# Rows and bases of matmul operands moved to multiples of 256 bytes in a one-layer hybrid decoder step

## The chip, the core and the metric

The kernel runs on one core of a Trainium2 chip. The metric is the device time of one execution in microseconds (us), lower is better. Engines are named as the profile names them: PE is TensorE's matmul, PEld its weight load, DVE is VectorE, ACT is ScalarE, POOL is GpSimd, SP is the engine that issues most DMAs.

## What is computed

One inference step of one layer of a decoder whose heads fall into three groups, for 256 prompt tokens and 8 sample tokens that are handled together (T = 264 columns):

```python
D_MODEL = 4096                       # D_IN = 13324, D_MIX = 4096
P = rmsnorm(h) @ W_in                # one combined projection
A: sliding-window attention (12 heads, 4 kv heads, window 128, sinks, ALiBi), times silu(z_a)
B: mLSTM matrix memory (6 heads, chunks of 64), per-head RMS norm, output gate, times silu(z_m)
C: chunked spatial gating u * (tril(W_s) v + b), times silu(z_c)
h = h + concat(A, B, C) @ W_out
y = rmsnorm(h) ; states of A, B and C are outputs too
```

Almost all of the arithmetic is in the two projections. They are multiplied in float32 precision: each operand is split into a high and a low part of type fp32r, and three of the four products are summed.

## The kernel before

**Tiling.** The 4096 rows of the contraction are 32 tiles of 128 partitions (KT = 32). The tokens, transposed, are the moving operand: tile `xh` holds the high parts and `xl` the low parts, each `[128, 32, 264]`, so that row `k` of either is 264 consecutive fp32r values (1056 bytes) in every partition. The weights are the stationary operand. The output columns are worked on in 34 groups of 512 columns (26 of `W_in`, then 8 of `W_out`). In a group the contraction goes in 16 steps `c` of two rows (KK = 2): rows 2c and 2c+1. Each step has a weight tile of 128 x 1024 values, which `load_w` (L214) brings into a buffer `wf` by one DMA of 512 KB on SP's queue, four steps ahead. `split_w` (L223), two steps ahead, makes `wh` (ACT) and `wl = wf - wh` (DVE) of it. `wf`, `wh` and `wl` have three buffers each.

**The matmuls.** In the main loop (L989) each step runs 24 matmuls: for four column tiles `j`, for the two rows, three products into the accumulator `mp` of that column tile.

```python
for j in range(4):
    for kk in range(KK):
        k = KK * c + kk
        s = slice(P * j, P * j + P)
        PE.matmul(out, wh[:, kk, s], xh[:, k], ...)   # the first argument after out is stationary
        PE.matmul(out, wh[:, kk, s], xl[:, k], ...)
        PE.matmul(out, wl[:, kk, s], xh[:, k], ...)
```

Each matmul streams 264 columns past a stationary block of 128 x 128, and each has a weight load of its own. There are 34 x 16 x 24 = 13056 of them. The profile shows them as `mp<-xh,wh`, `mp<-xl,wh` and `mp<-xh,wl`: the moving operand stands first.

**Around them.** The work of the three head groups is written as generators that the main loop resumes between column tiles (`tick`); what they put on PE are some 700 small matmuls and transposes in plain fp32. The order on every engine is that of the program text; the scheduler's own reordering is off. At the end of each group the accumulators are read by ACT and DVE (`evac`). After the last group, a norm factor is formed and `finish` (L1067) scales the result on DVE and POOL and writes it out.

**Memory.** The pool `const` (L94) hands out addresses in the order of the calls: `xh`, `xl`, `yb` (the tokens in fp32, later the residual), `sms` (small constants, among them the identity for transposes), `ones`, `rstd`, `acc` and some narrow ones. The pool with `wf`, `wh` and `wl` lies behind it. In front of everything lie 16384 bytes of scratch for DMAs whose descriptors are made on the chip by software, and a few constants. Nearly all instructions stand under line 201 in the profile, which is a helper that records every operation; they are told apart by their tiles.

Where the operands of the 13056 matmuls begin, in bytes from the start of a partition, in the built program:

| operand | begins at | one row or block further | position within 256 bytes |
|---|---|---|---|
| `xh`, row k | 16512 | + 1056 per row | (128 + 32 k) mod 256 |
| `xl`, row k | 50304 | + 1056 per row | (128 + 32 k) mod 256 |
| `wh`, three buffers | 137248 | + 2048 per kk, + 512 per j | 32, always |
| `wl`, three buffers | 149536 | + 2048 per kk, + 512 per j | 32, always |

So the two rows of a step stand at 128 and 160 in steps 0, 4, 8 and 12 of a group, at 192 and 224 in steps 1, 5, 9 and 13, at 0 and 32 in steps 2, 6, 10 and 14, and at 64 and 96 in steps 3, 7, 11 and 15.

Of the kernel before, what the change touches and what calls it, by code (L numbers as in the profile page):

```python
# [10 lines left out]
F32 = mybir.dt.float32  # L11
F32R = mybir.dt.float32r
# [6 lines left out]
P = 128  # L19
D = 4096  # L20
KT = D // P
TP = 256
TS = 8
T = TP + TS
# [44 lines left out]
NWARM = 9  # L69
LAG = 6.0  # L70
NCH = KT // KK

SM = {}

# [14 lines left out]
def body(tc, xt, wi, wg, wo, sm, kc, vc, c0, wst, w00, bs, cgain, cbias,  # L89
         o_y, o_kv, o_cp, o_mp, o_cs, o_ms, o_cvp, o_cvs):  # L90
    nc = tc.nc
    from contextlib import ExitStack
    with ExitStack() as ctx:
        cp = ctx.enter_context(tc.tile_pool(name="const", bufs=1))  # L94
# [27 lines left out]
        ph.switch()  # L122
        keep = Phase("keep")

        xh = cp.tile([P, KT, T], F32R, name="xh")
        xl = cp.tile([P, KT, T], F32R, name="xl")
        yb = cp.tile([P, KT, T], F32, name="yb")
        sms = cp.tile([P, NSM], F32, name="sms")
        ones = cp.tile([P, P], F32, name="ones")
        epsc = cp.tile([P, 2], F32, name="epsc")  # L130
        epsc2 = cp.tile([P, 1], F32, name="epsc2")
        rstd = cp.tile([P, T], F32, name="rstd")
        acc = cp.tile([P, KK, T], F32, name="acc")

        def sc(name, i=0, n=None, rows=slice(None)):
# [74 lines left out]

        steps = [(g, c) for g in range(NG + NGO) for c in range(NCH)]
        wf_t, wh_t, wl_t = {}, {}, {}
# [23 lines left out]
        def load_x(s):  # L236
            if s < NCH:
                nc.sync.dma_start(yb[:, KK * s:KK * s + KK, :], xt[:, KK * s:KK * s + KK, :])

        def split_x(s):  # L240
            if s >= NCH:
                return
            for k in range(KK * s, KK * s + KK):
                if s == 0:
                    V.tensor_scalar(xh[:, k], yb[:, k], sc("ng", k), None, ALU.mult)
                else:
                    A.activation(xh[:, k], yb[:, k], AF.Copy, scale=sc("ng", k))
                V.scalar_tensor_tensor(xl[:, k], yb[:, k], sc("ng", k), xh[:, k].bitcast(F32),
                                       ALU.mult, ALU.subtract)

        SQ = [6, 7, 8, 9] + [s for s in range(NCH) if s not in (6, 7, 8, 9)]

        def square_x(n):

            if n >= NCH:
                return
# [732 lines left out]
        for n, (g, c) in enumerate(steps):  # L989
# [24 lines left out]
            for j in range(4):  # L1014
                tick()
                out = main_ps[j][:, :T]
                for kk in range(KK):
# [4 lines left out]
                    PE.matmul(out, wl[:, kk, s], xh[:, k], start=False, stop=(k == KT - 1))  # L1022
                if c == NCH - 1:
                    if g < NG:
# [151 lines left out]
```

## Time and profile before

| | |
|---|---|
| runs of the kernel | 1704.19 us median of three (1701.7 to 9350.31) |
| the profiled execution | 1703.58 us, its span 1701.9 us |
| mean granted TensorE clock | 0.994 |
| busy: PE, PEld | 1678.2 us, 1662.2 us |
| busy: DVE, ACT, POOL | 909.4 us, 739.2 us, 80.7 us |
| read from HBM, written | 314.20 MB, 12.60 MB: 192 GB/s over the span |

The span runs from the first to the last instruction that the profile records; the execution's own time is 1.7 us longer. A row of a group gives the instruction with its tiles and shapes, how many there are, their busy time and the mean of one, and the idle time ahead of them. The end of a matmul in the profile is modelled, and a row's duration (0.28 us) overlaps that of the next matmuls, so the pace is read from the starts. In the views in order of time the first column is the start in us from the start of the span, the second the duration.

### The profile page before, as it was taken

How to read it: one execution, taken by the hardware profiler on the slowest of the kernel's cores; microseconds unless marked ns; L12 is line 12 of the kernel's file. 1: busy time of each engine (PE TensorE's matmuls, PEld its weight loads, DVE VectorE, ACT ScalarE, POOL GpSimd, SP SyncE). 2: the span in 40 equal slices, each digit the busy share in tenths (PEclk: the TensorE clock that was granted, in tenths of full speed). 3: DMA queues.
4: the chain of work that ended last, by engine and by line, in shares of the span. 5: the costliest groups of instructions: out<-in, count | busy, mean ns of one | idle time of the engine just before them, and what ended most of it. 6: DMA issues, size and time to landing. Idle time of an engine off the chain costs nothing.

```text
span 1701.9 us, 32534 instructions
## 1 busy us (share of the span) xinstructions
PE 1678.2 (99%) x13754; PEld 1662.2 (98%) x13754; DVE 909.4 (53%) x1277; ACT 739.2 (43%) x971; POOL 80.7 (5%) x82
## 2 busy tenths in 40 slices
PE   9999999999999999999999999999999999999995
PEld 9999999999999999999999999999999999999995
DVE  6555644555544455555555665444666554444445
ACT  6554433444434343444344444334454444344442
POOL 0000000000000000001001100000100120000002
PEclk9999999999999999999999999999999999999998
DMA  8555558545455555667767666555656655555553
GB/s 297 169 177 175 185 185 276 157 157 162 149 173 176 183 177 183 203 202 234 228 212 240 214 223 216 180 180 180 206 176 221 206 185 188 186 177 183 177 182 145
DMA packets 102177, 328.91 MB, mean 193 GB/s; under 512 B 11090, under 2 KB 24328, under 8 KB 102032
## 3 DMA queue, kind: packets, MB, share of 16 engines
q1 hardware_dynamic: 101072, 326.04, 59.8%
q8 instruction: 107, 1.75, 0.4%
q10 hardware_dynamic: 960, 0.81, 0.1%
q14 instruction: 38, 0.31, 0.0%
HBM read 314.20 MB, written 12.60 MB: 192 GB/s over the span
## 4 chain that ended last, share of the span: by engine, by line
PE 97%; DVE 1%; DMA 1%; ACT 0%; issue 0%; SPq 0%; DVEq 0%; ACTq 0%
PE mp L201 93%; PE mx L201 3%; DVE yb L201 1%; DMA wf<-wo 1%; PE sn L201 0%; DVE wl L201 0%; DMA wf<-wi 0%; PE gps L201 0%; ACT wh L201 0%; DVE rstd L201 0%; DVE TM L201 0%; DVE mvs L201 0%; ACT L201 0%; DVE es L201 0%; SPq L973 0%
## 5 line engine op out<-in xcount | busy, mean ns | idle before, releaser
L201 PE MATMUL mp<-xh,wh 128*128 128x264 f32 x4352 | 1250.4, 287 | 1.7 <-ACT wh L201 1.1
L201 PE MATMUL mp<-xh,wl 128*128 128x264 f32 x4352 | 1238.8, 285 | 2.6 <-DVE wl L201 2.6
L201 PE MATMUL mp<-xl,wh 128*128 128x264 f32 x4352 | 1237.4, 284 | 0.0
L201 DVE TENSOR_TENSOR wl<-wf,wh 128x1024 fp32r<-128x1024 f32 (+1 forms) x545 | 686.4, 1263 | 756.8 <-ACT wh L201 750.4
L201 ACT ACTIVATE wh<-wf 128x1024 fp32r<-128x1024 f32 (+1 forms) x545 | 575.1, 1058 | 823.8 <-PE mp L201 737.5
L201 PEld LDWEIGHTS mp<-xh,wh 128*128 128x128 f32 x4352 | 819.7, 188 | 8.1 <-issue 5.5
L201 PEld LDWEIGHTS mp<-xh,wl 128*128 128x128 f32 x4352 | 819.9, 188 | 3.5 <-DVE wl L201 3.5
L201 PEld LDWEIGHTS mp<-xl,wh 128*128 128x128 f32 x4352 | 819.9, 188 | 0.4
L201 POOL TENSOR_TENSOR acc<-acc,es 128x264 f32<-128x264 f32 x29 | 21.9, 755 | 417.1 <-ACT es L201 415.1
L201 POOL TENSOR_SCALAR_AFFINE_SELECT tmp<-bc 128x128 f32<-128x128 f32 x12 | 5.5, 482 | 495.8 <-DMA bc<-gd 495.8
L201 ACT ACT_TABLE_LOAD x22 | 28.2, 1283 | 1.2 <-PEq L1156 0.8
L201 ACT ACTIVATE es<-yb 128x264 f32<-128x264 f32 x37 | 15.3, 412 | 17.7 <-DVE yb L201 17.7
L201 POOL TENSOR_TENSOR cb<-cb,bc 128x2056 f32<-128x2056 f32 x6 | 21.7, 3616 | 0.0
L201 ACT ACTIVATE bias<-bias,ar 128x128 f32<-128x128 f32 (+1 forms) x24 | 10.8, 448 | 24.9 <-DVE ar L201 24.8
L201 POOL MEMSET pad<- 128x1024 f32 x2 | 1.9, 950 | 413.7 <-PE mx L201 413.7
L201 DVE SCALAR_TENSOR_TENSOR cb<-vb,wsk,cb 128x257 f32<-128x257 f32 x48 | 20.1, 480 | 0.0
L201 ACT ACTIVATE es<-et 128x264 f32<-128x264 f32 x32 | 12.6, 419 | 17.1 <-DVE yb L201 13.9
L201 ACT ACTIVATE xh<-yb 128x264 fp32r<-128x264 f32 x32 | 12.1, 412 | 17.7 <-DVE yb L201 17.7
L201 DVE TENSOR_TENSOR et<-mp,rstd 128x264 f32<-128x264 f32 x52 | 18.8, 423 | 0.0
L201 ACT ACTIVATE yb<-yb,sms 128x264 f32<-128x264 f32 x32 | 16.5, 517 | 1.0
L201 DVE TENSOR_TENSOR yb<-yb,rstd 128x264 f32<-128x264 f32 x32 | 16.1, 558 | 0.0
L201 DVE SCALAR_TENSOR_TENSOR xl<-yb,sms,xh 128x264 fp32r<-128x264 f32 x32 | 14.4, 489 | 0.8 <-ACT xh L201 0.8
(177 smaller groups left out, 461.6 us busy)
## 6 DMA issues: line engine op xcount, KB each, us to landing
wf<-wi SPq DMA_DIRECT2D x415, 512.0 KB, 3.4
wf<-wo SPq DMA_DIRECT2D x128, 512.0 KB, 3.4
cb<-c SPq DMA_DIRECT2D x12, 514.0 KB
o_cs<-cb SPq DMA_DIRECT2D x12, 514.0 KB, 6.2
vb<-vsd SPq DMA_DIRECT2D x12, 512.0 KB, 4.8
yb<-xt SPq DMA_DIRECT2D x34, 132.0 KB, 3.5
yb<-xt SPq DMA_DIRECT2D x15, 264.0 KB, 7.1
o_y<-yb SPq DMA_DIRECT2D x7, 528.0 KB, 3.3
```

The source lines that it names most:

```text
L201: return fn(*a, **k)
```

## The change

Each row of `xh` and `xl` is given 320 values of room (1280 bytes, five times 256), of which the first 264 are used: the tile is `[128, 32, 320]` and the kernel keeps a view of 264 columns. Two small tiles that nothing reads or writes, of 128 and 96 bytes, are put in front of `xh` and in front of `acc`. The scratch for DMAs shrinks from 16384 to 1024 bytes, which makes room for the two larger tiles. `yb`, `mp` and all other tiles keep their shapes.

```diff
+ROW = 320
+PAD0, PAD1 = 32, 24
...
-        xh = cp.tile([P, KT, T], F32R, name="xh")
-        xl = cp.tile([P, KT, T], F32R, name="xl")
+        cp.tile([P, PAD0], F32, name="pad0")
+        xh = cp.tile([P, KT, ROW], F32R, name="xh")[:, :, :T]
+        xl = cp.tile([P, KT, ROW], F32R, name="xl")[:, :, :T]
         yb = cp.tile([P, KT, T], F32, name="yb")
...
         rstd = cp.tile([P, T], F32, name="rstd")
+        cp.tile([P, PAD1], F32, name="pad1")
         acc = cp.tile([P, KK, T], F32, name="acc")
...
-    nc = _bacc.Bacc("TRN2", target_bir_lowering=False, num_devices=1)
+    nc = _bacc.Bacc("TRN2", target_bir_lowering=False, num_devices=1, dynamic_dma_scratch_size=1024)
```

No instruction is added, removed or moved: every engine has the same operations in the same order and shapes. What changes are addresses. In the built program afterwards:

| operand | begins at | one row or block further | position within 256 bytes |
|---|---|---|---|
| `xh`, row k | 1280 | + 1280 per row | 0, always |
| `xl`, row k | 42240 | + 1280 per row | 0, always |
| `wf`, `wh`, `wl`, three buffers each | 124160, 136448, 148736 | + 2048 per kk, + 512 per j | 0, always |

`yb` moves from 84096 (128 within 256 bytes) to 83200 (0), `wf` from 32 to 0, `ones` from 0 to 128, the identity in `sms` from 232 to 104. The tiles of the head groups, behind these, all move down by 800 bytes and so stand 32 bytes lower within 256 than before (224 becomes 192, 96 becomes 64).

## The prediction

> **What bounds the kernel now.** I read the page's table of busy times first, then the groups of instructions, then the chain that ended last.
>
> ```profile
> span 1701.9 us, 32534 instructions
> PE 1678.2 (99%) x13754; PEld 1662.2 (98%) x13754; DVE 909.4 (53%) x1277; ACT 739.2 (43%) x971; POOL 80.7 (5%) x82
> ...
> PE 97%; DVE 1%; DMA 1%; ACT 0%; issue 0%; SPq 0%; DVEq 0%; ACTq 0%
> ...
> L201 PE MATMUL mp<-xh,wh 128*128 128x264 f32 x4352 | 1250.4, 287 | 1.7 <-ACT wh L201 1.1
> L201 PE MATMUL mp<-xh,wl 128*128 128x264 f32 x4352 | 1238.8, 285 | 2.6 <-DVE wl L201 2.6
> L201 PE MATMUL mp<-xl,wh 128*128 128x264 f32 x4352 | 1237.4, 284 | 0.0
> L201 DVE TENSOR_TENSOR wl<-wf,wh 128x1024 fp32r<-128x1024 f32 (+1 forms) x545 | 686.4, 1263 | 756.8 <-ACT wh L201 750.4
> L201 ACT ACTIVATE wh<-wf 128x1024 fp32r<-128x1024 f32 (+1 forms) x545 | 575.1, 1058 | 823.8 <-PE mp L201 737.5
> ```
>
> PE is busy nearly all the time, the chain lies on it for 97% of the span, and its three large groups wait for almost nothing (1.7, 2.6 and 0.0 us). The two engines that feed it are idle for long: ACT waits 737.5 us for PE to free a weight buffer. So the time is the number of matmuls, 3 x 4352 = 13056, times the pace at which PE starts them, and some 100 us of other work. The pace is not the mean of 284 to 287 ns, because successive matmuls overlap. It is read from a long undisturbed piece of the chain:
>
> ```profile
> 482.59 265.10 PE mp L201 x2172
> ```
>
> 265.10 us over 2172 matmuls are **122.0 ns** each, and 13056 x 0.1220 = 1593 us of the 1701.9. Nothing else in this kernel is worth a tenth of that, so the question is whether these 122.0 ns depend on addresses. For that I cut a quiet piece (in a group of the output projection, past its first steps) at the starts of four successive steps, which take their two rows of x from different places within 256 bytes: 128 and 160, then 192 and 224, then 0 and 32, then 64 and 96. The columns are the window, its length, PE's busy time and the matmuls that touch it (24 start in each), the clock and the share of DMA.
>
> ```profile
> 1548.04:1551.02 2.98, 2.98 (x26) 1.00 0.57 187
> 1551.02:1553.93 2.91, 2.91 (x26) 1.00 0.59 186
> 1553.93:1556.83 2.90, 2.90 (x26) 1.00 0.56 181
> 1556.83:1559.75 2.92, 2.92 (x26) 1.00 0.59 180
> ```
>
> The same 24 matmuls take 2.98, 2.91, 2.90 and 2.92 us: 124.2, 121.2, 120.8 and 121.7 ns each. The clock is full in all four and DMA alike, and the weights stand at 32 within 256 in all four. So the place of x costs up to 3 ns in 122, and at the worst place (128 and 160) the pace is the slowest. That much the trace shows. Within the third step the rows alternate in threes, and the first matmul of each three shows how long a row holds PE:
>
> ```profile
> 1553.93 0.28 PE L201 MATMUL mp<-xh,wh 128*128 128x264 f32 x1
> ...
> 1554.30 0.28 PE L201 MATMUL mp<-xh,wh 128*128 128x264 f32 x1
> ...
> 1554.66 0.28 PE L201 MATMUL mp<-xh,wh 128*128 128x264 f32 x1
> ...
> 1555.02 0.28 PE L201 MATMUL mp<-xh,wh 128*128 128x264 f32 x1
> ...
> 1555.38 0.29 PE L201 MATMUL mp<-xh,wh 128*128 128x264 f32 x1
> ...
> 1555.75 0.28 PE L201 MATMUL mp<-xh,wh 128*128 128x264 f32 x1
> 1555.88 0.28 PE L201 MATMUL mp<-xl,wh 128*128 128x264 f32 x1
> 1555.99 0.28 PE L201 MATMUL mp<-xh,wl 128*128 128x264 f32 x1
> 1556.12 0.28 PE L201 MATMUL mp<-xh,wh 128*128 128x264 f32 x1
> ...
> 1556.48 0.28 PE L201 MATMUL mp<-xh,wh 128*128 128x264 f32 x1
> ...
> 1556.84 0.29 PE L201 MATMUL mp<-xh,wh 128*128 128x264 f32 x1
> ```
>
> The row at 0 holds PE from 1553.93, 1554.66, 1555.38 and 1556.12 for 0.37, 0.36, 0.37 and 0.36 us, 121.7 ns per matmul. The row at 32 does so from 1554.30, 1555.02, 1555.75 and 1556.48 for 0.36, 0.36, 0.37 and 0.36 us, 120.8 ns, and three of the four give 120.0.
>
> **The change part by part.** *x at 0 instead of all eight places.* Two readings of these rows give two answers. If the place of x alone counts, all rows will run as the row at 0 does: 121.7 instead of 122.0 ns, a gain of 0.3 x 13056 = 4 us. If what counts is how x stands to the weight block that PE loads beside it, then the row at 32 is the one to look at: the weights are at 32 too, the difference is 0, and after the change it is 0 for every matmul (x at 0, weights at 0). I take the second, because the row with difference 0 is the quickest in its step and the step with the largest differences (96 and 128) the slowest. Between 120.0 and 120.8 I take 120.4: a gain of 1.6 x 13056 = **21 us**.
>
> *Weights at 0 instead of 32.* The trace of before has every main weight block at 32, so it shows nothing of this. By the nearest rows, those of x's places, a place is worth between 1.2 ns less (120.8) and 2.2 ns more (124.2) than the mean, so between -16 and +29 us. I take nothing for it, because with the difference held at 0 I have no row for either sign, and keep both ends for the range.
>
> *The small matmuls.* The remaining matmuls of PE, 13754 - 13056 = 698, have operands that move down by 32 within 256 bytes. At the largest spread seen, 3.4 ns, that is 2 us either way. I take 0.
>
> *DVE, ACT and DMA.* They read and write at other addresses: `wf` and `yb` now begin at 0. Whatever that does to `wl` (1263 ns) or `wh` (1058 ns) is hidden under a step of 2900 ns on PE: both have more idle time ahead of them than they are busy. DVE's 909.4 us are 1.7 us a step, so it would have to grow by over a microsecond a step before PE waited for it. In the first group the DMAs are near their limit:
>
> ```profile
> 20.00:40.00 20.00, 20.00 (x166) 20.00 (x166) 14.71 (x22) 14.03 (x24) 0.00 (x0) 1.00 0.94 321
> ```
>
> PE is busy in all 20 us there with DMA at a share of 0.94. A gain of 1.6 ns in 122 would ask for 1.3% more, which fits; a gain of 7 ns would not, and would be lost for the 16 steps of that group (16 x 24 x 7 ns = 2.7 us).
>
> *The smaller scratch.* The page lists DMA issues from SP and ACT alone, with the weights the largest group:
>
> ```profile
> q1 hardware_dynamic: 101072, 326.04, 59.8%
> ...
> wf<-wi SPq DMA_DIRECT2D x415, 512.0 KB, 3.4
> wf<-wo SPq DMA_DIRECT2D x128, 512.0 KB, 3.4
> ```
>
> None has descriptors that software makes, so nothing uses the scratch: 0, and no DMA that could run short of it.
>
> **Sum.** 1703.58 of the profiled execution - 21 = **1682 us**, 1.2% less. The profiled execution stands 0.6 us under the median of the runs, 1704.19, which is nothing beside the terms.
>
> **What a page says against it.** The Trainium skill, "SBUF — State Buffer", section "Who interferes with whom", gives PE two read ports of its own, one for the moving operand and one for weight loads, and says that PE never waits on anyone. By that no address matters and the time stays at 1704. The four windows above speak against it: with equal clock and DMA they differ by 0.08 us in 2.9 with the place of x alone.
>
> **The rivals.** *No change.* It would be so if the eight places of x are phases of one pattern whose mean of 122.0 ns is set by something else, such as the load of a weight block that each matmul needs. For it: no step comes out under 120.8 ns, and single gaps that are shorter are paid back by the next. At 121.7 to 122.0 ns the time is 1700 to 1704 us.
>
> *Faster by much.* The differences between places might be what is left of a stall that is present at all of them, and that only vanishes when x and weights both begin at 0. For it: in the row at 32 the gap from its second matmul to its third, 1555.88 to 1555.99, is 0.11 us; the second is the one of the three that has matmuls of its own row on both sides, and so the nearest thing to the stream after the change. Against it: the gaps beside it are 0.13, as if they paid for it. If 115 ns (between 0.11 and 0.12) became the pace, the gain is 7.0 x 13056 = 91 us, or 88 without the first group: 1615 us. It is faster by over 2% (34 us, 2.6 ns) from a pace of 119.4 ns down.
>
> The Trainium skill, "TensorE: Matmul & The Clock Gate", section "Back-to-back issue gap", gives N / 2.4 + 2.5 ns for isolated matmuls; at N = 264 that is 112.5, an estimate by which this rival would reach 1580 us. No stretch of this trace runs at that pace.
>
> *Slower.* With everything at 0, each matmul's read of x starts at the same place as the weight block that is read beside it, and if both are served by the same part of the memory, the collision comes in every matmul in the same way rather than in some. The rows at 128 and 160 show what a bad phase costs when it does not go away:
>
> ```profile
> 1549.53 0.29 PE L201 MATMUL mp<-xh,wh 128*128 128x264 f32 x1
> ...
> 1549.91 0.28 PE L201 MATMUL mp<-xh,wh 128*128 128x264 f32 x1
> ```
>
> 0.38 us for three, 126.7 ns: 4.7 x 13056 = 61 us more, 1765 us. At the pace of that whole step (124.2) it would be 29 us, 1732. Against it: the row at 32 has difference 0 already and is not slow. It decides from 124.6 ns on. About 2% is what a measurement of this kernel can tell from no change.
>
> **How the numbers follow.** Forecast (pace 119.4 to 121.6, 1670 to 1699 us): 0.44. No change (1699 to 1710): 0.11. Faster by much (under 1670): 0.33. Slower (over 1710): 0.12, of which a third stays within 2%. So faster by over 2% is 0.33 and 2 in 100 that the forecast is just too small, 0.35; slower by over 2% 0.08; within 2% the other 0.57. The predicted time is that of the forecast, 1682 us. The range has to take in most of the fast case and part of the slow one: from 1610, which is just under a pace of 115, to 1725, which covers a step's pace of 123.6. Outside I leave about 0.1 below and 0.08 above.
>
> **What would show it.** In the profile after, the steps of a quiet stretch would all be equally long, at 24 x 120.4 ns = 2.89 us, instead of 2.98, 2.91, 2.90 and 2.92 in turn. If they are equal at 2.92 or more, place counts but my choice of row was wrong. If they still alternate by fours, x's place was never the cause. Equal steps of 2.76 or less are the fast rival, 2.99 or more the slow one. DVE's and ACT's idle times should shrink by the gain and no DMA wait should appear on PE outside the first group. The prediction is wrong if the place of the weight block has an effect of its own, which no row of before can show, or if equal places make a stable pattern that the mixed sequence never reached.

## The result, and the profile after

The changed kernel takes **1690.01 us** in the median of four runs (1687.46 to 1692.27), against 1703.86 us for the kernel before in the same session: a ratio of **0.992**, 95% interval 0.990 to 0.994. That is 14 us or 0.8% less: within 2%, but clear of zero. The forecast was 1682. One of the four runs of the kernel before took 9350 us; it is left out of the ratio.

The page of the profile after (span, busy times, the large groups; the line numbers are four higher):

```profile
span 1687.7 us, 32534 instructions
PE 1663.3 (99%) x13754; PEld 1646.4 (98%) x13754; DVE 911.6 (54%) x1277; ACT 739.1 (44%) x971; POOL 80.9 (5%) x82
...
L205 PE MATMUL mp<-xh,wh 128*128 128x264 f32 x4352 | 1242.5, 286 | 2.5 <-ACT wh L205 1.9
L205 PE MATMUL mp<-xh,wl 128*128 128x264 f32 x4352 | 1231.3, 283 | 2.6 <-DVE wl L205 2.5
L205 PE MATMUL mp<-xl,wh 128*128 128x264 f32 x4352 | 1230.9, 283 | 0.0
L205 DVE TENSOR_TENSOR wl<-wf,wh 128x1024 fp32r<-128x1024 f32 (+1 forms) x545 | 685.3, 1261 | 741.1 <-ACT wh L205 734.5
L205 ACT ACTIVATE wh<-wf 128x1024 fp32r<-128x1024 f32 (+1 forms) x545 | 574.9, 1057 | 808.6 <-PE mp L205 712.1
```

The span is 14.2 us shorter, PE is busy 14.9 us less, and hardly anything else has moved: DVE's and ACT's busy times (within 2.2 us), their durations for `wl` and `wh`, and PE's waits are as before. The idle time ahead of `wl` and `wh` is shorter by 15.7 and 15.2 us. The same long undisturbed piece of the chain as before, 2172 matmuls, gives the pace:

```profile
478.24 262.90 PE mp L205 x2172
```

262.90 / 2172 = 121.0 ns instead of 122.0. How it comes about is seen in windows cut at the starts of successive steps, first in one group of the output projection, then in the next (24 matmuls start in each window):

```profile
1488.74:1491.62 2.88, 2.88 (x26) 1.00 0.70 218
1491.62:1494.50 2.88, 2.88 (x26) 1.00 0.62 188
1494.50:1497.38 2.88, 2.88 (x26) 1.00 0.58 182
...
1535.04:1537.95 2.91, 2.91 (x27) 1.00 0.61 200
1537.95:1540.86 2.91, 2.91 (x27) 1.00 0.60 186
1540.86:1543.77 2.91, 2.91 (x26) 1.00 0.57 180
```

The repeat after four steps is gone. But there are now two paces: 2.88 us a step (120.0 ns) in one group, 2.91 (121.3 ns) in the next, with the same instructions, addresses and clock. Over the whole trace, of the 469 steps that hold no small matmuls, some 200 take 2.88 us and some 220 take 2.91 or 2.92; the rest begin a group or wait. The order in time shows what the slower pace is:

```profile
1535.64 0.28 PE L205 MATMUL mp<-xh,wl 128*128 128x264 f32 x1
1535.77 0.28 PE L205 MATMUL mp<-xh,wh 128*128 128x264 f32 x1
1535.88 0.28 PE L205 MATMUL mp<-xl,wh 128*128 128x264 f32 x1
1536.01 0.28 PE L205 MATMUL mp<-xh,wl 128*128 128x264 f32 x1
1536.13 0.29 PE L205 MATMUL mp<-xh,wh 128*128 128x264 f32 x1
1536.25 0.28 PE L205 MATMUL mp<-xl,wh 128*128 128x264 f32 x1
1536.38 0.28 PE L205 MATMUL mp<-xh,wl 128*128 128x264 f32 x1
1536.49 0.28 PE L205 MATMUL mp<-xh,wh 128*128 128x264 f32 x1
```

The gaps, from starts rounded to 0.01 us, are 0.13, 0.11, 0.13, 0.12, 0.12, 0.13, 0.11: a pattern of five (126, 124, 116, 120 and 121 ns in turn, to within a nanosecond or so) that goes on until something interrupts PE. In the quicker groups the five are replaced by gaps of 120 ns, or by four of 123, 122, 120 and 115 ns, whose mean is 120.0 too. The trace changes from one pattern to the other only at the start of a group or at a step that waits or holds small matmuls. What decides which one comes next is not shown.

### The profile page after: what moved, and what is told of

It is laid out like the page before. It is cut to its first block, busy times and chain, and to the rows that moved or that the text cites. A ratio compares the mean times of both kernels' runs of the same rounds, so it can differ in the third digit from the quotient of the medians.

```text
span 1687.7 us, 32534 instructions
## 1 busy us (share of the span) xinstructions
PE 1663.3 (99%) x13754; PEld 1646.4 (98%) x13754; DVE 911.6 (54%) x1277; ACT 739.1 (44%) x971; POOL 80.9 (5%) x82
## 4 chain that ended last, share of the span: by engine, by line
PE 96%; DVE 2%; DMA 1%; ACT 1%; issue 0%; SPq 0%; DVEq 0%; ACTq 0%
PE mp L205 92%; PE mx L205 3%; DVE wl L205 1%; DVE yb L205 1%; DMA wf<-wo 1%; PE sn L205 0%; ACT wh L205 0%; DMA wf<-wi 0%; PE gps L205 0%; DVE rstd L205 0%; DVE TM L205 0%; ACT es L205 0%; DVE mvs L205 0%; ACT L205 0%; ACT yb L205 0%
## 5 line engine op out<-in xcount | busy, mean ns | idle before, releaser
L205 ACT ACTIVATE es<-yb 128x264 f32<-128x264 f32 x37 | 15.2, 412 | 17.7 <-DVE yb L205 17.7
L205 DVE TENSOR_TENSOR xl<-yb,xh 128x264 fp32r<-128x264 f32 x32 | 12.7, 429 | 3.9 <-ACT xh L205 3.9
```

Of the source, the lines that this page charges most:

```text
L205: return fn(*a, **k)
```

## The experiments

Three theories stood against each other. Theory 1: the difference between the place of x and that of the weights within 256 bytes counts. Theory 2: the place of x alone counts. Theory 3: there is a floor of 120.0 ns, and places only choose a repeating pattern of gaps at or above it.

**A map of places.** A kernel that leaves out the whole layer and runs only stretches of 120 matmuls, with x and weights at each of eight places. `stretch` issues 120 matmuls, the three products in turn; `brk` issues two or three small matmuls as a break:

```diff
+        for rep in range(2):
+            for a in range(8):
+                for b in range(8):
+                    brk(2 if rep == 0 else 3)
+                    stretch(f"x{32 * a}w{32 * b}q", 120, T, P, 8 * a, 8 * b)
```

> None of the layer is computed: only PE runs, in stretches of 120 matmuls shaped as the large ones (264 columns, 128x128 weights, three products in turn), x at one of eight places within 256 bytes and the weights at one of eight, 64 pairs, each twice with a different break ahead. Theory 1 (the difference between the place of x and that of the weights counts): pairs with equal difference have equal pace, the difference 0 gives 120.0 to 121.4 ns, the difference 96 about 124.5. Theory 2 (the place of x alone counts): the pace depends on x and not on the weights, with x at 0 at 121.5. Theory 3 (the pace is a floor of 120.0 ns, and the place only decides into which repeating pattern of start gaps PE falls): many pairs give 120.0, a pair may give 120.0 in one of its stretches and 121.4 in the other, and none is below 120.0.

The chain of waits shows each stretch as a piece: start, length, and the name, which has the places of x and of the weights. The first eight:

```profile
9.05 14.56 PE x0w0q L127 x120
...
24.06 14.41 PE x0w32q L127 x120
...
38.92 14.43 PE x0w64q L127 x120
...
53.80 14.60 PE x0w96q L127 x120
...
68.84 14.80 PE x0w128q L127 x120
...
84.08 15.20 PE x0w160q L127 x120
...
99.72 14.51 PE x0w192q L127 x120
...
114.68 14.67 PE x0w224q L127 x120
```

With x at 0 throughout, the weights alone move the pace from 14.41 to 15.20 us per 120. So theory 2 falls. The other places of x give much the same numbers, one place further along. The pace after the first 20 matmuls of each stretch, by difference, over all 16 stretches that share it:

| x minus weights, mod 256 | pace in ns (stretches) |
|---|---|
| 0 | 121.3 to 121.4 (10), 120.0 (6) |
| 32 | 122.2 (16) |
| 64 | 120.9 to 121.0 (15), 120.0 (1) |
| 96 | 126.7 (12), 121.6 to 121.7 (3), 120.0 (1) |
| 128 | 123.3 (11), 120.0 (5) |
| 160 | 121.7 (16) |
| 192 | 120.0 (16) |
| 224 | 120.0 (16) |

Theory 1 holds in so far as the difference says which paces can come, and the price that it gave the difference 96, about 124.5 ns, was too small. Of theory 3 the floor holds as well: nothing is below 120.0, and four differences have more than one pace, so equal differences do not always run equally. The difference 0, that of the change, is one of the four. The same pair of places can have either pace, as two of them show, the first stretch of each ahead of the second:

```profile
144.90 14.41 PE x32w32q L127 x120
...
505.90 15.18 PE x128w32q L127 x120
...
1111.36 14.56 PE x32w32q L127 x120
...
1477.26 14.60 PE x128w32q L127 x120
```

The mean of the eight upper values is 122.0 ns, the pace of the kernel before.

**Columns and weight widths.** The same frame, with x and weights at 0, and other sizes:

```diff
+        for rep in range(3):
+            for N in (232, 248, 256, 264, 272, 280, 288, 304, 320, 384, 512):
+                brk(2 + rep)
+                stretch(f"n{N}m128q", 120, N, P, 0, 0)
+            for M in (32, 64, 96, 112):
+                brk(2 + rep)
+                stretch(f"n264m{M}q", 120, T, M, 0, 0)
```

> None of the layer is computed: stretches of 120 matmuls with x and weights at 0 within 256 bytes, three times each: 232 to 512 columns with 128-column weights, then 264 columns with weights of 32 to 112 columns. If the streaming of x sets the floor of 120.0 ns, the pace falls with the columns (232 columns 13 ns below 264) and does not change with the width of the weights. If the weight load sets it, 232 to 264 columns all take 120.0, columns count only from about 282 on (at 0.417 ns per column), and narrower weights at 264 columns bring the pace down to about 110 to 113 ns.

```profile
8.84 13.40 PE n232m128q L127 x120
...
22.69 13.60 PE n248m128q L127 x120
...
36.73 14.39 PE n256m128q L127 x120
...
51.57 14.56 PE n264m128q L127 x120
...
131.06 17.59 PE n320m128q L127 x120
...
170.36 27.25 PE n512m128q L127 x120
...
198.05 14.40 PE n264m32q L127 x120
```

Fewer columns of x are quicker (13.40 / 120 = 111.7 ns at 232). Narrower weight blocks are not quicker than the floor: those of 32 to 112 columns all run at 120.0 ns, where the full block ran at 121.3 in its three stretches. They lose the slower pattern and no more. So the floor is not the duration of the weight load; it goes with the number of columns of x. Whether it is the read of x or the writing of the result, which has as many columns, these stretches do not tell apart. The floor is no straight line either: from 248 to 256 columns the pace rises by 6.6 ns, from 256 to 264 by 1.4.

**The difference 0 at another place.** The first padding is enlarged, so that x and weights all stand at 32.

```diff
-PAD0, PAD1 = 32, 24
+PAD0, PAD1 = 40, 24
```

> As the changed kernel, but x and the weights all at 32 within 256 bytes instead of 0. Theory 1 (the difference counts): the same as the changed kernel, ratio to before 0.992. Theory 2 (the place of x alone counts, as the row at 32 in the kernel before, 120.3 ns): 0.987. Theory 3 (floor and patterns): between 0.985 and 0.993, by which pattern the groups fall into.

Ratio to before 0.992 (0.991 to 0.994), 1690.48 us: the time of the changed kernel (1690.01) again. Multiples of 256 bytes have no merit of their own.

**The wider rows in the worst place.** Rows 1280 bytes apart, but x at 128 and the weights at 32, which is where they come to lie without the two paddings:

```diff
-PAD0, PAD1 = 32, 24
+PAD0 = 64
...
-        cp.tile([P, PAD1], F32, name="pad1")
```

> As the changed kernel, but all rows of x at 128 within 256 bytes and the weights at 32, the pair that was slowest in the kernel before (steps of 2.98 us, its row at 128 about 124.9 ns). Theories 1 and 2 both: 124 to 125 ns, ratio to before 1.015 to 1.022. Theory 3 (the slow steps came from the mixing of places, and equal places fall into a pattern near the floor): 0.985 to 1.00.

Ratio 1.027 (1.025 to 1.029), 1751.06 us. The long piece of the chain, two steps of one of its groups, and one of a late group:

```profile
492.83 275.11 PE mp L204 x2172
```

```profile
522.30:525.34 3.04, 3.04 (x26) 1.00 0.60 172
525.34:528.38 3.04, 3.04 (x26) 1.00 0.62 172
...
1540.80:1543.72 2.92, 2.92 (x26) 1.00 0.66 191
```

275.11 / 2172 = 126.7 ns, the upper value of the map for the difference 96. This is above the 124 to 125 ns that I had expected from the kernel before, whose rows hold the difference for three matmuls only. As in the map it is not the only pace of this difference: of the 469 steps without small matmuls some 315 take 3.04 us, some 95 take 2.92 and 25 take 2.88, the last two kinds mostly in groups near the end. The traced execution, 1744.0 us, was also the quickest of the four; the others took 1750.5 to 1751.9. Equal rows alone can cost more than they can gain: 48 us here, against 22 in the best case below.

**Other differences in the full kernel.** The weights at 32 (difference 224) and at 64 (192), x at 0. The edit of the first is shown; the second has 40 in place of the last 32:

```diff
-PAD0, PAD1 = 32, 24
+PAD0, PAD1 = 32, 32
```

> As the changed kernel, but with the weights at 32 within 256 bytes (x stays at 0), so that the difference x minus weights is 224 for every matmul. Theory 1 with the map of places: the one pattern of exactly 120.0 ns, every quiet step 2.88 us instead of a mixture of 2.88 and 2.91, about 12 us less than the changed kernel: 1677 us, ratio to before 0.984. If the changed kernel's gain came from having all operands at multiples of 256, this is slower than it: 0.993 to 1.00.

> As the changed kernel, but with the weights at 64 (difference 192). Theory 1 with the map: 120.0 ns in every quiet step, 1677 us, ratio 0.984, the same as with the weights at 32. If multiples of 256 count: 0.993 to 1.00.

Ratios 0.988 (0.986 to 0.989) at 1681.79 us and 0.989 (0.987 to 0.990) at 1683.13 us. Both beat the changed kernel, 0.992 (0.990 to 0.994). With the weights at 32 the long piece of the chain and two steps, at the place in the group where the changed kernel had 2.91:

```profile
475.85 261.18 PE mp L205 x2172
```

```profile
1527.69:1530.57 2.88, 2.88 (x26) 1.00 0.63 176
1530.57:1533.45 2.88, 2.88 (x26) 1.00 0.75 220
```

120.3 ns with the starts of the groups in it, 2.88 us in the steps: the one pace, as the map has it. The gain over the changed kernel is 8 us where I had expected 12. I had counted a gain for all 544 steps. But some 200 steps of the changed kernel ran at 2.88 already, and only the 220 or so at 2.91 and 2.92 could gain: 0.03 us each, 7 us. The 74 steps that hold small matmuls gave 1 us more.

**One part at a time.** The bases and the scratch of the change without its wider rows, and the scratch alone:

```diff
-ROW = 320
+ROW = T
```

> The bases and the scratch of the changed kernel without its wider rows: rows of x lie 1056 bytes apart as before, xh, xl and the weights begin at 0 within 256 bytes, so the difference runs through all eight values. Theory 1: the mean over the eight differences, 122.0 with the upper values of the map (120.9 with its lower ones), quiet steps that repeat every four, ratio 0.993 to 1.00, and 1.00 if the patterns are those of the kernel before. If aligned bases or aligned weights were worth something by themselves: as the changed kernel, 0.992 or less.

Ratio 0.998 (0.997 to 0.999), 1699.25 us; the long piece of the chain is

```profile
481.16 264.60 PE mp L205 x2172
```

121.8 ns. The difference runs through all eight values again, in other pairs, and of the 14 us of the change 4 are left. Of aligned bases as such nothing shows beyond what another mixture might give. Four steps in a row of a quiet group have the differences 0 and 32, 64 and 96, 128 and 160, 192 and 224:

```profile
1496.87:1499.78 2.91, 2.91 (x27) 1.00 0.63 183
1499.78:1502.71 2.93, 2.93 (x26) 1.00 0.66 193
1502.71:1505.63 2.92, 2.92 (x26) 1.00 0.60 180
1505.63:1508.55 2.92, 2.92 (x26) 1.00 0.62 180
```

By the map's upper values they would take 2.92, 2.97, 2.94 and 2.88 us. The last is not the quickest. So where the difference changes every three matmuls, a difference does not cost what it costs in a steady stream; the map's mean fits the whole, its single values do not.

```diff
-    nc = _bacc.Bacc("TRN2", target_bir_lowering=False, num_devices=1)
+    nc = _bacc.Bacc("TRN2", target_bir_lowering=False, num_devices=1, dynamic_dma_scratch_size=1024)
```

> The kernel before with 1024 instead of 16384 bytes of scratch and nothing else: all addresses move by 60 times 256, so that every place within 256 bytes stays. All theories: no change, 1.00, steps of 2.98, 2.91, 2.90 and 2.92 us as before. A difference would mean that the scratch or the address beyond 256 bytes counts.

Ratio 1.000 (0.999 to 1.001), 1703.51 us.

**Does the read of the weight block collide?** The slow differences with narrower blocks, in the frame of the map:

```diff
+            for d in (32, 96, 128, 160, 224):
+                for M in (32, 64, 96, 128):
+                    brk(2 + rep)
+                    stretch(f"d{d}m{M}q", 120, T, M, d // 4, 0)
+                brk(2 + rep)
+                stretch(f"d{d}n248q", 120, 248, P, d // 4, 0)
```

> None of the layer is computed: stretches of 120 matmuls of 264 columns at five of the differences between the place of x and that of the weights (32, 96, 128, 160, 224), each with weight blocks 32, 64, 96 and 128 columns wide, and a stretch with 248 columns of x; every stretch twice. If the slow pairs come from x's read meeting the read of the next weight block, narrower blocks end them: at 32 columns all differences give 120.0 ns, and at 128 the map's 122.2, 126.7, 123.3, 121.7 and 120.0 come back. If the place of x relative to something that does not shrink with the block (the start of the load alone) counts, the width changes nothing.

The names have the difference and the width of the block:

```profile
83.43 14.77 PE d96m32q L127 x120
98.65 14.41 PE d96m64q L127 x120
...
128.35 15.18 PE d96m128q L127 x120
...
306.60 14.40 PE d224m32q L127 x120
321.45 14.78 PE d224m64q L127 x120
...
351.91 14.41 PE d224m128q L127 x120
```

At 128 columns the map's values came back; otherwise neither expectation came. The width does change which differences are slow: at 96 the blocks of 128 and 32 columns are slow (126.7 and 123.3 ns) and those of 64 and 96 are not (120.0); at 224 it is the other way round (120.0, and 123.3 at 64 and 96). But a block of 32 columns does not end it. With 248 columns of x the difference counts as well, from 113.3 ns at 160 to 116.3 at 96. So the width of the weight block has a part in it, but where and how the load and the stream of x get into each other's way stays open.

## Why the prediction was right, and where its sizes were off

*The bound.* Right: PE's pace times 13056, and no other engine came into the sum.

*The difference and not the place of x.* Right. It was the choice on which the sum rested; the map shows it with x fixed, and x at 32 with weights at 32 shows it in the full kernel (0.992 both times). The ground for the choice was weaker than the choice. It was that the row with the difference 0 was the quickest in its step. The other row of that step, x at 0, has the difference 224, and that one runs at 120.0 ns in every stretch of the map. It looked slow only in the mixture. The largest differences are not the slowest either: 192 and 224 are the quickest, and 160, as far from 0 as 96 the other way round, costs 121.7 and not 126.7. So there was luck in it that these rows pointed the right way.

*1.6 ns per matmul.* The sign was right, the size too large: the long piece fell by 1.0 ns, and 1.0 x 13056 = 13 us is about what the span lost (14.2). The term that was mis-sized is the pace after, 120.4 ns from the row at 32. Four runs of 0.36 and 0.37 us could not tell that a steady difference 0 has two paces, 120.0 and 121.3. In the 425 steps that are undisturbed in both traces the mean went from 121.9 to 120.7 ns, and the long piece, which has the starts of groups in it, from 122.0 to 121.0. The sum had taken its 122.0 from the long piece and its 120.4 from undisturbed matmuls. The steps are equal within a stretch without interruption, as forecast, but at 2.88 or at 2.91, not at 2.89. One of the prediction's own signs of being wrong thus came in part: equal places make stable patterns. That the slower one of the difference 0 costs only 1.3 ns above the floor was not to be seen before; had it been like that of 96, the kernel would have been slower.

*Weights at 0, taken as nothing.* Right: x at 32 with the weights at 32 runs as x at 0 with the weights at 0.

*Small matmuls, DVE, ACT, DMA and scratch at nothing.* Right for the scratch, which was measured alone (1.000). The others were not run alone. The page after shows the same durations for `wl` and `wh`, and the 14.2 us of the span less 13 of the pace leave no room for more than a microsecond or two.

*"PE never waits on anyone".* The rule of the Trainium skill, "SBUF — State Buffer", section "Who interferes with whom", by which the prediction had it that nothing would change, does not cover what happens here: with x and everything else fixed, the place of the weights moves PE's pace from 120.0 to 126.7 ns. Whether PE waits at these ports or elsewhere, no run here shows.

*The rivals.* "No change" had the right observation, that short gaps are paid back by the next, and gave the pace to the weight load, which the runs with narrower blocks and with fewer columns refute. "Faster by much" rested on the gap of 0.11 us; such gaps are part of repeating patterns (116 among 126, 124, 120 and 121), and no difference of the map runs below 120.0. "Slower" named the price of a bad phase that does not go away, 126.7 ns, and that is what the difference 96 mostly costs when all rows have it. It gave that price to equal places, and there it was wrong: equal places are the difference 0.

## What to carry to other kernels

Where PE's pace is the bound, read it from the starts of the matmuls and group them by the place of their operands within 256 bytes; a pace that repeats with the row pitch is a sign. Then fix the difference between the moving and the stationary operand instead of aligning both: here, with 264 columns of x and 128 of weights, 192 or 224 gave 120.0 ns in every stretch of the map, 0 gave 120.0 or 121.3, and 96 up to 126.7. Other shapes want a map of their own: with weight blocks of 64 columns the difference 224 ran at 123.3 and 96 at 120.0. An equal pitch makes the difference constant, but it decides nothing until the bases are placed too: the same wider rows gave 0.988, 0.992 and 1.027.

## What the runs showed of the hardware that was not expected

A stream of equal matmuls has more than one steady pattern at four of the eight differences: in the map the difference 128 ran at 123.3 ns in 11 stretches and at 120.0 in 5. In the trace of the changed kernel the patterns change only where something interrupts the stream, but the break does not decide by its length alone: after the same three small matmuls the difference 128 ran at either pace. A few starts therefore do not give the pace of a long stream.

The pace is not proportional to the columns: 113.3 ns at 248 (13.60 us per 120; 114.9 in one stretch of three), 120.0 at 256, 146.7 at 320 and 226.7 at 512. From 256 on these multiples of 64 fit 26.7 ns for each 64 columns and 13.3 more for each matmul; between 256 and 320 the stretches lie below that line (131.7 at 288). The 8 sample columns on top of 256 cost between nothing and 1.3 ns.
